# MoE down projection: high and low activation parts side by side for experts with at most 64 tokens, and a branch around the third pass

## The chip, the core and the metric
The kernel runs on one core of one Trainium2 chip. The metric is the time of one execution on the device in microseconds; the time before is 1982.52 us, the median of 3 runs (1981.83 to 1983.2). Engines are named as the profile names them: PE is TensorE's matmul side and PEld its weight loads, DVE is VectorE, ACT is ScalarE, POOL is GpSimd, SP issues the DMAs.

## The reference, cut to what matters
Two layers of a diffusion backbone work on 256 latent tokens (and 256 context tokens) of width 1024. The last step of the second layer is a mixture of experts, on the latent tokens alone. Each token goes to its two best of 8 experts; each expert is a SwiGLU with 3584 hidden units:

```
logits = h @ router_w + router_b
top_v, top_i = lax.top_k(logits, 2)
top_p = softmax(top_v)
combine = sum(one_hot(top_i, 8) * top_p[..., None], -2)
for e in range(8):
    y = y + combine[:, e:e+1] * ((silu(h @ w_gate[e]) * (h @ w_up[e])) @ w_down[e])
```

All of it is float32. The 256 tokens give 512 token-expert pairs. With the inputs of the reference the experts 0 to 7 get 56, 67, 72, 33, 73, 39, 115 and 57 tokens.

## The kernel before
**Splitting.** A float32 product is made of three TensorE passes on operands of type fp32r. Each operand is split into a high part (a copy in fp32r) and a low part (the rest): `split` (lines 135 to 145) does this for weights, with ACT writing `wh` (line 142) and DVE writing `wl` (line 144). `three` (lines 156 to 160) then issues high x high, high x low and low x high into one PSUM tile. The activations are the stationary operand, the weights the moving one (512 columns).

**Buffers.** Weights come in chunks of 1 MB. `rawtile` hands out the raw buffers in a fixed cycle of nine (six `rawx`, two `raw`, one half of `hT`); SP's queue holds the loads in program order, each waiting until its buffer is free. A chunk gives two weight pairs (`wh`, `wl`). Pairs live in seven buffers each of `wh` and `wl`, used in turn (three in `whp` and `wlp`, four in `mowx`).

**The expert loop.** `moe` (line 956) routes: `pc` holds the number of tokens of each expert on every partition, `pos` the place of each token in its expert's list, or -1. `gather_x` (line 1025) builds `Gr`, a 0/1 matrix (token by place) from a comparison of `pos` with a row of places, and brings the tokens of two experts at a time into places 0 to 127 by matmuls with it; `gather_g` turns `Gr` over for the way back (`gt`) and fetches the combination weights (`cw`). A token's row goes to each place whose column of `Gr` holds a 1. `experts` (line 1132) then runs over 8 experts and 7 blocks of 512 hidden units, 56 blocks in all. A block is:

- the up product `pu` (`wblock`: 4 pairs, 24 matmuls), `Silu` of the gate product on ACT (line 1158) and its product with `pu` on DVE (`sg`, line 1159);
- the gate product of the next block (`wblock`, 24 matmuls), in the middle of which (`MID`) `hidden` (line 1079) transposes `sg` by 4 matmuls and splits it into `hx`: high part on ACT (line 1086), low part on DVE (line 1087);
- `down` (line 1090): 4 pairs, each used by 6 matmuls (three passes for each half of the 1024 output columns), into two PSUM tiles `dn` that are kept over the 7 blocks.

After an expert's last block `scatter` (line 1111) evicts `dn` with the weights `cw`, as high and low part `ye` (ACT line 1117, DVE line 1118), and brings it back to token order by 16 matmuls with `gt` (line 1125), which DVE adds into `hT` (line 1128); these are spread over the next block.

An expert with more than 128 tokens would need a second turn: line 1021 loads the largest count into a register of every engine and line 1022 runs the whole loop again inside a conditional if it is over 128. With these inputs it is skipped.

**What sets the order.** The program is written in text order; a planner of the tile framework then orders the instructions of each engine's queue by a timing model of its own, and adds the semaphores. So the queues differ from the text: the transposes of `hidden` may stand earlier than `MID` says, and weight halves of later blocks ahead of an eviction. A conditional is a unit to the planner: nothing from outside is interleaved with what is in it, and the text behind it becomes a new stretch with its own order, on every engine. On the skipping path each engine with work inside waits until its earlier work is counted as finished, and then adds what the skipped work would have counted. Each engine runs its own queue in order, without a common clock.

Of the kernel before, what the change touches and what calls it, by code (L numbers as in the profile page):

```python
# [9 lines left out]
F32 = mybir.dt.float32  # L10
F32R = mybir.dt.float32r
I32 = mybir.dt.int32
AF = mybir.ActivationFunctionType
OP = mybir.AluOpType
# [3 lines left out]
P = 128  # L18
# [3 lines left out]
LAT = 256  # L22
# [3 lines left out]
NE = 8  # L26
FFE = 3584
NB = FFE // 512
CW = 31
EPS = 1e-6  # L30
PADW = 286

C_ID, C_ONE, C_UT, C_IO, C_TJ, C_HALF = 0, 128, 256, 384, 640, 644
CSTW = 648
# [38 lines left out]
class Kernel:  # L73
# [44 lines left out]
    def mm(self):  # L118
        return self.psm.tile([P, 512], F32, name="mm", tag="mm")
# [594 lines left out]
            nc.vector.tensor_tensor(r, od, r, OP.mult)  # L714
            nc.vector.tensor_tensor(yt[1][:, 2 + c, y0:y0 + 256], r[:, 0:256], r[:, 256:512], OP.add)

    MID = 5
    WCYC = 3
    CUTS = ((0, 256), (256, 512))
    ORDER = ("crgp0SBqmt1b23M", "kcrgp0SBqt123")  # L720
# [235 lines left out]
    def moe(self):  # L956
        nc = self.nc
# [4 lines left out]
        W = self.small  # L962
# [19 lines left out]
        ps = self.tp()  # L982
# [4 lines left out]
        pc = self.po()  # L987
# [1 line left out]
        nc.tensor.matmul(pc[:, 0:96], self.ones, selp[:, 1], start=False, stop=True)  # L989
        nc.vector.scalar_tensor_tensor(t1, ps[:, 0:192].rearrange("p (t n) -> p t n", t=2)[:, :, 0:NE], 1.0, sel, OP.add, OP.mult)  # L990
        nc.vector.tensor_scalar(pos, t1, -1.0, None, OP.add)
        self.pos = pos
        utp = self.pool(self.ctx, "utp", 1)
        uth = utp.tile([P, 2, D], F32R, name="uth")
        utl = utp.tile([P, 2, D], F32R, name="utl")
# [29 lines left out]
    def gather_x(self, ep, chunk, first=False):  # L1025
        nc = self.nc
        xh, xl = self.u8((P, KT, 2, P), F32R, "xh"), self.u8((P, KT, 2, P), F32R, "xl")
        Gr = self.mos.tile([P, 2, 256], F32R, name="Gr", bufs=1)
        iota = self.cst[:, C_IO + chunk * P:C_IO + (chunk + 1) * P]
        for i in range(2):  # L1030
            for t in range(2):
                nc.vector.tensor_scalar(Gr[:, t, i * P:(i + 1) * P], iota, self.pos[:, t, ep + i:ep + i + 1], None, OP.is_equal)

        def step(q):
            ps = self.dn() if first and q % 2 else self.tp()
            for r in range(2):
                c = slice(r * 256, r * 256 + 256)
                k = 2 * q + r
                for j, ut in enumerate((self.uth, self.utl)):
                    for t in range(2):  # L1040
                        nc.tensor.matmul(ps[:, c], ut[:, t, k * P:(k + 1) * P], Gr[:, t, :], start=j + t == 0, stop=j + t == 2)
                b = self.mcol(1, 24 + k, 0)
                v = ps[:, c].rearrange("p (i n) -> p i n", i=2)
                nc.scalar.activation(xh[:, k], v, AF.Identity, bias=b)
                nc.vector.scalar_tensor_tensor(xl[:, k], v, b, xh[:, k].bitcast(F32), OP.add, OP.subtract)

        steps = [lambda q=q: step(q) for q in range(4)]
        return [(xh[:, :, i], xl[:, :, i]) for i in range(2)], Gr, steps
# [27 lines left out]
                    mid()  # L1076
        return ps

    def hidden(self, g):
        nc = self.nc  # L1080
        tp = self.tp()
        for f in range(4):
            nc.tensor.transpose(tp[:, f * P:(f + 1) * P], g[:, f * P:(f + 1) * P], self.ident)
        hx = self.mos.tile([P, 2, 4, P], F32R, name="hx", tag="hx", bufs=1)
        t3 = tp.rearrange("p (f n) -> p f n", f=4)
        nc.scalar.copy(hx[:, 0], t3)  # L1086
        nc.vector.tensor_tensor(hx[:, 1], t3, hx[:, 0].bitcast(F32), OP.subtract)  # L1087
        return hx

    def down(self, e, b, pd, hx):  # L1090
        hh, hl = hx[:, 0], hx[:, 1]
        end = e == NE - 1 and b == NB - 1
        w = []

        def part(j, f, n):
            wh, wl = w[2 * j + f]
            c = slice(n * 512, n * 512 + 512)
            self.three(pd[n], hh[:, 2 * j + f], hl[:, 2 * j + f], wh[:, 0, c], wl[:, 0, c],
                       b == 0 and j == 0 and f == 0, b == NB - 1 and j == 1 and f == 1)

        for j in range(2):
            w += self.weights(self.A["w_moed"][e, 2 * b + j], (2, D))
            for f in range(2):
                for n in range(1 if end else 2):
                    part(j, f, n)
        if end:
            for j in range(2):
                for f in range(2):
                    part(j, f, 1)

    def scatter(self, pd, G, last):
        nc = self.nc
# [19 lines left out]
    def experts(self, chunk, first=None):  # L1132
# [22 lines left out]
        for n, (e, b) in enumerate(blocks):  # L1155
            pu = self.wblock(X[e], e, b, 1)
            g = self.sg.tile([P, 512], F32, name="sg")
            nc.scalar.activation(g, pg, AF.Silu)
            nc.vector.tensor_tensor(g, g, pu, OP.mult)
            hx = []  # L1160
            for f in later[0:2]:
                f()
            if e % 2 and b == 1 and e + 1 < NE:
                gather = prep(e + 1)
            if b:
                next(gather, None)
            if n + 1 < len(blocks):
                e1, b1 = blocks[n + 1]
                pg = self.wblock(X[e1], e1, b1, 0, lambda: hx.append(self.hidden(g)))
            else:  # L1170
                hx.append(self.hidden(g))
            for f in later[2:4]:
                f()
            later = []
            if b == 0:
                pd = [self.dn() for _ in range(2)]
            self.down(e, b, pd, hx[0])
            if b == NB - 1:
                later = self.scatter(pd, G[e], e == NE - 1)
        for f in later:  # L1180
# [112 lines left out]
```

## Time and profile before
| | |
|---|---|
| median of 3 runs | 1982.52 us |
| profiled execution: span from first to last instruction | 1977.4 us |
| TensorE busy (share of the span) | 1909.9 us (97%) |
| DVE, ACT busy | 1472.1 us (74%), 1065.3 us (54%) |
| expert loop | from about 957 us to the end |
| down matmuls (`dn<-wh,hx`, `dn<-wl,hx`, `dn<-wh,hx`) | 3 x 448 |

The profiled execution is one of its own, told by its span; what the runs' times hold beside the span is the start and the end of the program. The page gives busy times, the stage tables split them by stretches of time, the timelines list instructions in order of time with their start, duration and line, and what an engine sat idle for stands in brackets with the engine that released it. A matmul's record lasts longer than the distance to the next one, because matmuls are pipelined: distances between starts tell the pace.

### The profile page before, as it was taken

How to read it: one execution, taken by the hardware profiler on the slowest of the kernel's cores; microseconds unless marked ns; L12 is line 12 of the kernel's file. 1: busy time of each engine (PE TensorE's matmuls, PEld its weight loads, DVE VectorE, ACT ScalarE, POOL GpSimd, SP SyncE). 2: the span in 40 equal slices, each digit the busy share in tenths (PEclk: the TensorE clock that was granted, in tenths of full speed). 3: DMA queues.
4: the chain of work that ended last, by engine and by line, in shares of the span. 5: the costliest groups of instructions: out<-in, count | busy, mean ns of one | idle time of the engine just before them, and what ended most of it. 6: DMA issues, size and time to landing. Idle time of an engine off the chain costs nothing.

```text
span 1977.4 us, 24739 instructions
## 1 busy us (share of the span) xinstructions
PE 1909.9 (97%) x9422; PEld 1517.8 (77%) x9422; DVE 1472.1 (74%) x1930; ACT 1065.3 (54%) x1371; POOL 106.6 (5%) x98
## 2 busy tenths in 40 slices
PE   5999999999999999999899999999999999999996
PEld 2886548878878789877788888888878888788785
DVE  4875344785545358756799999889898898988986
ACT  3322334332222234435678777767776777767773
POOL 2100011110110020011000000000000000000000
PEclk9999999999999999999999999999999999999998
DMA  8220355455544213226698999998999999999991
GB/s 313 101 94 25 132 198 217 162 213 192 189 151 156 79 60 133 96 74 250 233 367 324 336 348 346 349 352 328 346 342 364 368 339 341 340 356 368 348 367 52
DMA packets 71806, 481.97 MB, mean 244 GB/s; under 512 B 8320, under 2 KB 12544, under 8 KB 14464
## 3 DMA queue, kind: packets, MB, share of 16 engines
q1 hardware_dynamic: 71680, 480.32, 65.1%
q8 instruction: 76, 1.25, 0.3%
q14 instruction: 50, 0.41, 0.1%
HBM read 479.24 MB, written 1.05 MB: 243 GB/s over the span
## 4 chain that ended last, share of the span: by engine, by line
issue 53%; PE 43%; DVE 2%; POOL 1%; ACT 1%; DMA 0%; POOLq 0%; SPq 0%; DVEq 0%; ACTq 0%
PE mm L159 9%; PE mm L158 9%; PE mm L160 9%; PE dn L158 2%; PE dn L160 2%; PE dn L159 2%; PE po L553 2%; PE dn L540 1%; PE mm L207 1%; PE tp L549 1%; PE dn L685 1%; DVE wl L144 1%; POOL rms L706 1%; PE dn L564 0%; PE tp L372 0%
## 5 line engine op out<-in xcount | busy, mean ns | idle before, releaser
L144 DVE TENSOR_TENSOR wl<-rawx,wh 128x1024 fp32r<-128x1024 f32 x496 | 586.7, 1221 | 87.8 <-ACT wh L142 84.7
L142 ACT CAST wh<-rawx 128x1024 fp32r<-128x1024 f32 x496 | 497.2, 1049 | 182.3 <-PE mm L159 92.6
L159 PE MATMUL mm<-wl,xh 128*128 128x512 f32 x896 | 356.1, 397 | 0.0
L158 PE MATMUL mm<-wh,xh 128*128 128x512 f32 x896 | 354.8, 396 | 0.0
L160 PE MATMUL mm<-wh,xl 128*128 128x512 f32 x896 | 352.3, 393 | 0.0
L142 ACT CAST wh<-raw 128x1024 fp32r<-128x1024 f32 x220 | 224.1, 1050 | 192.8 <-PE mm L159 106.8
L144 DVE TENSOR_TENSOR wl<-raw,wh 128x1024 fp32r<-128x1024 f32 x220 | 263.0, 1224 | 49.7 <-ACT wh L142 47.6
L158 PE MATMUL mm<-uh,wh 128*128 128x512 f32 (+1 forms) x664 | 245.2, 372 | 4.7 <-ACT uh L396 3.6
L159 PE MATMUL mm<-ul,wh 128*128 128x512 f32 (+1 forms) x664 | 244.8, 371 | 1.0 <-POOL ul L397 0.5
L160 PE MATMUL mm<-uh,wl 128*128 128x512 f32 (+1 forms) x664 | 244.3, 370 | 0.0
L159 PEld LDWEIGHTS mm<-wl,xh 128*128 128x128 f32 x896 | 168.6, 188 | 40.3 <-DVE wl L144 3.3
L158 PEld LDWEIGHTS mm<-wh,xh 128*128 128x128 f32 x896 | 168.5, 188 | 36.6
L160 PEld LDWEIGHTS mm<-wh,xl 128*128 128x128 f32 x896 | 168.6, 188 | 36.3
L159 PE MATMUL dn<-wl,hx 128*128 128x512 f32 x448 | 177.4, 396 | 2.2 <-DVE wl L144 2.2
L160 PE MATMUL dn<-wh,hx 128*128 128x512 f32 x448 | 172.7, 393 | 0.3 <-DVE hx L1087 0.3
L158 PE MATMUL dn<-wh,hx 128*128 128x512 f32 x448 | 160.0, 396 | 0.7 <-ACT hx L1086 0.7
L158 PEld LDWEIGHTS mm<-uh,wh 128*128 128x128 f32 x664 | 126.0, 191 | 33.4 <-ACT uh L396 5.3
L159 PEld LDWEIGHTS mm<-ul,wh 128*128 128x128 f32 x664 | 126.1, 191 | 25.8 <-POOL ul L397 2.1
L160 PEld LDWEIGHTS mm<-uh,wl 128*128 128x128 f32 x664 | 126.1, 191 | 22.0 <-issue 1.1
L159 PEld LDWEIGHTS dn<-wl,hx 128*128 128x128 f32 x448 | 84.3, 188 | 23.5 <-DVE wl L144 4.8
L158 PEld LDWEIGHTS dn<-wh,hx 128*128 128x128 f32 x448 | 84.2, 188 | 22.5 <-ACT hx L1086 4.1
L160 PEld LDWEIGHTS dn<-wh,hx 128*128 128x128 f32 x448 | 83.5, 188 | 19.3 <-DVE hx L1087 1.6
(289 smaller groups left out, 2602.9 us busy)
## 6 DMA issues: line engine op xcount, KB each, us to landing
rawx<-w_moe SPq DMA_DIRECT2D x148, 1024.0 KB, 6.8
rawx<-w_moed SPq DMA_DIRECT2D x72, 1024.0 KB, 6.7
raw<-w_moe SPq DMA_DIRECT2D x54, 1024.0 KB, 6.6
raw<-w_mod SPq DMA_DIRECT2D x29, 1024.0 KB, 4.9
rawx<-w_mod SPq DMA_DIRECT2D x19, 1024.0 KB, 5.5
raw<-w_moed SPq DMA_DIRECT2D x19, 1024.0 KB, 7.1
hT<-w_moed SPq DMA_DIRECT2D x18, 1024.0 KB, 6.8
hT<-w_moe SPq DMA_DIRECT2D x17, 1024.0 KB, 6.7
```

The source lines that it names most:

```text
L142: nc.scalar.copy(h, r)
L144: nc.vector.tensor_tensor(l, r, h.bitcast(F32), OP.subtract)
L158: mm(ps, ah, bh, start=first, stop=False)
L159: mm(ps, ah, bl, start=False, stop=False)
L160: mm(ps, al, bh, start=False, stop=last)
L207: nc.tensor.matmul(ps[32 * j:32 * j + 32, :], self.cT[:, k, :], w[:, j, :], start=start, stop=stop)
L540: nc.tensor.matmul(sc, self.qT[r0:r0 + 64, hp, q0 + qt * P:q0 + (qt + 1) * P], self.kT[r0:r0 + 64, hp, :], start=True, stop=True)
L549: nc.tensor.transpose(tp[:, kt * P:(kt + 1) * P], p[:, kt * P:(kt + 1) * P], self.ident)
L553: nc.tensor.matmul(po[r0:r0 + 64, 0:256], self.vt[:, kt, h * 64:h * 64 + 64], pt[:, kt, :], start=kt == 0, stop=kt == 3)
L685: nc.tensor.matmul(sc[:, t * 256:t * 256 + 256], self.rqk[r, 1, o0 + t * P:o0 + (t + 1) * P], self.rqk[r, 0, o0:o0 + 256], start=True, sto ...
L706: nc.gpsimd.tensor_tensor(m, m, self.half.unsqueeze(2).to_broadcast([P, 4, 2]), OP.pow)
```

## The change
The experts with at most 64 tokens (`few`) get each token twice, at place p and at place p + 64: the second half of `Gr`'s columns compares with `pos2 = pos + 64 * few`. In `hidden`, the upper 64 columns of the high part are then overwritten by t - few * high (`self.few` holds -few): for a small expert that is the low part, for a large one the sum with 0, the exact transposed value in fp32r. One stationary tile so holds high and low parts side by side; two passes (with `wh` and `wl`) give all products, and the scatter adds the two places of a token. The third pass (`rest`) is put behind the first 16 matmuls of a block and inside a conditional on TensorE alone, on the expert's count, which is loaded into a register once per expert. In the second turn (chunk 1) the third pass is always done. The special order of the very last block is dropped, and `MID` goes from 5 to 4.

```diff
-    MID = 5
+    MID = 4
...
-        self.pos = pos
+        few, pos2 = W("few", (NE,)), W("pos2")
+        nc.vector.tensor_scalar(few, pc[:, 0:NE], HALF + 0.5, None, OP.is_lt)
+        for t in range(2):
+            nc.vector.scalar_tensor_tensor(pos2[:, t], few, float(HALF), pos[:, t], OP.mult, OP.add)
+        self.pos = (pos, pos2)
+        self.few = W("nfew", (NE,))
+        nc.gpsimd.tensor_scalar(self.few, few, -1.0, None, OP.mult)
+        self.cnt8 = W("cnt8", (NE,), I32)
+        nc.vector.tensor_copy(self.cnt8, pc[:, 0:NE])
+        self.many = {}
...
-                nc.vector.tensor_scalar(Gr[:, t, i * P:(i + 1) * P], iota, self.pos[:, t, ep + i:ep + i + 1], None, OP.is_equal)
+                for h in range(2):
+                    c = slice(h * HALF, h * HALF + HALF)
+                    ps = self.pos[h if chunk == 0 else 0]
+                    nc.vector.tensor_scalar(Gr[:, t, i * P:(i + 1) * P][:, c], iota[:, c], ps[:, t, ep + i:ep + i + 1], None, OP.is_equal)
...
         nc.scalar.copy(hx[:, 0], t3)
+        if chunk == 0:
+            b = hx[:, 0, :, HALF:]
+            nc.vector.scalar_tensor_tensor(b, b.bitcast(F32), self.few[:, e:e + 1], t3[:, :, HALF:], OP.mult, OP.add)
         nc.vector.tensor_tensor(hx[:, 1], t3, hx[:, 0].bitcast(F32), OP.subtract)
...
-    def down(self, e, b, pd, hx):
+    def down(self, e, b, pd, hx, chunk):
...
             for f in range(2):
-                for n in range(1 if end else 2):
-                    part(j, f, n)
-        if end:
-            for j in range(2):
-                for f in range(2):
-                    part(j, f, 1)
+                wh, wl = w[2 * j + f]
+                for n in range(2):
+                    c = slice(n * 512, n * 512 + 512)
+                    k = 2 * j + f
+                    mm(pd[n], hh[:, k], wh[:, 0, c], start=b == 0 and k == 0, stop=False)
+                    mm(pd[n], hh[:, k], wl[:, 0, c], start=False, stop=b == NB - 1 and k == 3)
+
+        def rest():
+            for n in range(2):
+                for k in range(4):
+                    mm(pd[n], hl[:, k], w[k][0][:, 0, n * 512:n * 512 + 512], start=False, stop=True, skip_group_check=True)
+
+        if chunk:
+            rest()
+        else:
+            with self.tc.If(self.many[e] > HALF):
+                rest()
...
             if b == 0:
                 pd = [self.dn() for _ in range(2)]
+                if chunk == 0:
+                    self.many[e] = nc.tensor.value_load(self.cnt8[0:1, e:e + 1], min_val=0, max_val=LAT)
```

## Rows read from the trace of the kernel before

**Rows 1.** The page: busy us, share of the span and instructions of each engine.
```profile
PE 1909.9 (97%) x9422; PEld 1517.8 (77%) x9422; DVE 1472.1 (74%) x1930; ACT 1065.3 (54%) x1371; POOL 106.6 (5%) x98
```
**Rows 2.** The stage table, 800 us of the expert loop: busy us (instructions), PE clock, DMA share, GB/s.
```profile
1100.00:1900.00 800.00, 797.42 (x3622) 647.46 (x3621) 709.76 (x721) 584.63 (x664) 0.00 (x0) 1.00 0.93 349
```
**Rows 3.** Timeline of PE, one block: start us, us, engine, line, operation, count.
```profile
1306.06 0.40 PE L160 MATMUL mm<-wh,xl 128*128 128x512 f32 x1
...
1309.51 0.39 PE L160 MATMUL mm<-wh,xl 128*128 128x512 f32 x1
1309.74 0.64 PE L158 MATMUL dn<-wh,hx 128*128 128x512 f32 x2
...
1315.33 0.39 PE L158 MATMUL mm<-wh,xh 128*128 128x512 f32 x1
```
**Rows 4.** Timeline of DVE, the same block: idle us before it and its releaser in brackets.
```profile
1303.84 0.69 DVE L1159 TENSOR_TENSOR sg<-sg,mm 128x512 f32<-128x512 f32 x1 [1.49 <-PE mm L160]
1304.45 1.22 DVE L144 TENSOR_TENSOR wl<-rawx,wh 128x1024 fp32r<-128x1024 f32 x1
1305.58 2.35 DVE L144 TENSOR_TENSOR wl<-raw,wh 128x1024 fp32r<-128x1024 f32 x2
1307.85 0.68 DVE L1087 TENSOR_TENSOR hx<-tp,hx 128x512 fp32r<-128x512 f32 x1
1308.45 2.35 DVE L144 TENSOR_TENSOR wl<-raw,wh 128x1024 fp32r<-128x1024 f32 x2
1311.51 4.63 DVE L144 TENSOR_TENSOR wl<-rawx,wh 128x1024 fp32r<-128x1024 f32 x4 [0.70 <-ACT wh L142]
...
1321.03 0.69 DVE L1159 TENSOR_TENSOR sg<-sg,mm 128x512 f32<-128x512 f32 x1 [1.48 <-PE mm L160]
```
**Rows 5.** Groups by line, 1100 to 1900: busy us, mean ns, idle before and releaser.
```profile
L159 PE MATMUL dn<-wl,hx 128*128 128x512 f32 x356 | 141.3, 397 | 2.2 <-DVE wl L144 2.2
L1158 ACT ACTIVATE sg<-mm 128x512 f32<-128x512 f32 x44 | 26.3, 597 | 50.2 <-PE mm L160 50.2
```
**Rows 6.** Line 1022, the existing conditional: queue, operation, ns min/median/max, start.
```profile
L1022 PEldq COMPARE_BRANCH  x1: 3722/3722/3722, 1959.8 to 1959.8; - x1
...
L1022 DVEq COMPARE_BRANCH  x1: 72/72/72, 1960.8 to 1960.8; - x1
L1022 PEldq EVENT_SEMAPHORE  x1: 51/51/51, 1963.6 to 1963.6; - x1
```
**Rows 7.** Line 1021, the register load ahead of it, TensorE's queue.
```profile
L1021 PEldq TENSOR_LOAD <-cnti x1: 490/490/490, 1959.2 to 1959.2; - x1
```
**Rows 8.** Timeline of all engines, last block: TensorE stops for DVE and starts again.
```profile
1951.84 0.68 DVE L1087 TENSOR_TENSOR hx<-tp,hx 128x512 fp32r<-128x512 f32 x1
...
1952.58 0.50 PE L160 MATMUL dn<-wh,hx 128*128 128x512 f32 x1 [0.34 <-DVE hx L1087]
...
1952.91 0.39 PE L158 MATMUL dn<-wh,hx 128*128 128x512 f32 x1
```
**Rows 9.** Timeline of DVE, the change from expert 1 to expert 2.
```profile
1212.12 1.40 DVE L1118 SCALAR_TENSOR_TENSOR ye<-dn,cw,ye 128x512 fp32r<-128x512 f32 x2
...
1217.44 0.87 DVE L1128 SCALAR_TENSOR_TENSOR hT<-tp,mod,hT 128x256 f32<-128x256 f32 x2
```
**Rows 10.** Timeline of PE, scatter matmuls of the last expert.
```profile
1957.31 0.63 PE L1125 MATMUL tp<-gt,ye 128*128 128x256 f32 x4
```
**Rows 11.** Waits of SP's queue, 980 to 1950: us in total, times, longest.
```profile
SPq L132 <- DVE wl L144: 816.1, 314, 7.7
```
**Rows 12.** The page: DMA issues, KB each, median us from issue to landing.
```profile
rawx<-w_moe SPq DMA_DIRECT2D x148, 1024.0 KB, 6.8
```
**Rows 13.** Timeline of DVE, the end of the routing.
```profile
950.45 0.17 DVE L991 TENSOR_SCALAR pos<-t 128x16 f32<-128x16 f32 x1
```
**Rows 14.** Timeline of ACT, the change from expert 1 to expert 2.
```profile
1209.89 1.05 ACT L142 CAST wh<-rawx 128x1024 fp32r<-128x1024 f32 x1 [0.33 <-PE dn L160]
1210.85 1.26 ACT L1117 ACTIVATE ye<-dn,cw 128x512 fp32r<-128x512 f32 x2
```

More of the change, by code (lines that the diff above doesn't have):

```diff
@@ L31 @@
 PADW = 286
+HALF = 64
 C_ID, C_ONE, C_UT, C_IO, C_TJ, C_HALF = 0, 128, 256, 384, 640, 644
@@ L1077, in wblock, with hidden @@
         return ps
-    def hidden(self, g):
+    def hidden(self, g, e, chunk):
         nc = self.nc
@@ L1086, in hidden @@
         nc.scalar.copy(hx[:, 0], t3)
+        if chunk == 0:
+            b = hx[:, 0, :, HALF:]
+            nc.vector.scalar_tensor_tensor(b, b.bitcast(F32), self.few[:, e:e + 1], t3[:, :, HALF:], OP.mult, OP.add)
         nc.vector.tensor_tensor(hx[:, 1], t3, hx[:, 0].bitcast(F32), OP.subtract)
         return hx
-    def down(self, e, b, pd, hx):
+    def down(self, e, b, pd, hx, chunk):
+        mm = self.nc.tensor.matmul
         hh, hl = hx[:, 0], hx[:, 1]
-        end = e == NE - 1 and b == NB - 1
         w = []
[L1095 to L1099, printed above, removed]
         for j in range(2):
@@ L1168, in experts @@
                 e1, b1 = blocks[n + 1]
-                pg = self.wblock(X[e1], e1, b1, 0, lambda: hx.append(self.hidden(g)))
+                pg = self.wblock(X[e1], e1, b1, 0, lambda: hx.append(self.hidden(g, e, chunk)))
             else:
-                hx.append(self.hidden(g))
+                hx.append(self.hidden(g, e, chunk))
             for f in later[2:4]:
@@ L1176, in experts @@
                 pd = [self.dn() for _ in range(2)]
-            self.down(e, b, pd, hx[0])
+                if chunk == 0:
+                    self.many[e] = nc.tensor.value_load(self.cnt8[0:1, e:e + 1], min_val=0, max_val=LAT)
+            self.down(e, b, pd, hx[0], chunk)
             if b == NB - 1:
```

## Prediction, written before the result was known
> **What bounds the kernel now.** I read the page's busy times first, then the stage table, then one block of the expert loop on each engine, then the waits. TensorE is busy for 97% of the span [rows 1]. In the expert loop it is busy for 797.4 of 800 us at a granted clock of 1.00 (the 2.4 GHz level), VectorE (DVE) for 709.8, ScalarE (ACT) for 584.6, and the DMA engines for a share of 0.93 at 349 GB/s [rows 2]. So TensorE bounds this stage, but DVE has only 11% to give.
>
> One block (one expert, 512 of its hidden units) runs from one `sg` product to the next, 1303.84 to 1321.03: 17.19 us [rows 4]. TensorE never stops in it: gate and up matmuls start 0.230 us apart (15 starts from 1306.06 to 1309.51), down matmuls 0.233 us apart (24 from 1309.74 to 1315.33) [rows 3]. DVE follows: the low half of a weight pair takes 1.22 us, the next starts 1.135 us later; `sg` takes 0.61 us to the next start, the low half of `hx` 0.60. That makes 12 x 1.135 + 0.61 + 0.60 = 14.8 us of 17.19. The rest is idle at two places: 1.49 us ahead of `sg`, for a TensorE result, and 0.70 us ahead of the third down pair [rows 4]. TensorE waited 2.2 us in all for the down pass's low halves over 800 us [rows 5], so it runs close behind DVE there.
>
> **What the change does here.** The reference's router on its inputs gives the experts 56, 67, 72, 33, 73, 39, 115 and 57 tokens: four (0, 3, 5, 7) have at most 64 ("small"), four don't ("large").
>
> *Removed.* Each small expert drops 8 matmuls in each of 7 blocks: 4 x 7 x 8 = 224, x 0.233 = **-52.2 us**.
>
> *The branch.* The trace has one conditional. Its compare-and-branch takes 72 ns on DVE and 3722 ns on TensorE, where it jumps over a whole second expert loop; an event of 51 ns follows [rows 6]. The new jump passes 8 matmuls. On the skipping side the semaphore count of the skipped work has to be made up, which can only be done when the sixteenth matmul has ended, so the pipeline empties. A matmul lasts 0.39 us against a start every 0.23 (+0.16); after a wait TensorE starts 0.06 us behind its releaser (`hx` at 1951.84 + 0.68 = 1952.52, start 1952.58) and the second matmul comes 0.33 instead of 0.23 us later (+0.10) [rows 8]; the event adds 0.05 [rows 6], a short jump as much. Together 0.42; I take 0.45 x 28 = **+12.6 us**. Bounds: 0.1 (the emptying alone) and 3.7 us (each jump like the long one), 3 to 104 us. I stay near the low end because the target lies a few instructions ahead. The Trainium skill (Advanced Engine Details and Errata, Control Flow Timing) gives about 108 ns for a compare-and-branch and about 51 ns for a jump; with both exposed the term would be 28 x (0.37 + 0.16), an estimate of 14.8 us. The trace agrees only for DVE's short one; its long one is far slower. Large experts take the branch too, but TensorE's sequencer gets there while matmuls are queued: 0, at most 28 x 0.1. The eight register loads (490 ns [rows 7]) hide the same way: 0, at most 3.9.
>
> *DVE's new operation.* 56 times DVE rewrites the upper half of `hx` (128 x 256, from PSUM). The nearest row is line 1128's form, two in 0.87 us [rows 9], so about 0.40 each in a queue; ends 0.2 and 0.6: DVE's block becomes 15.2 us. A small block on TensorE becomes 17.19 - 8 x 0.233 + 0.45 = 15.8. So DVE still fits, with 0.6 us to spare instead of 2.4, and what matters is its queue order.
>
> *The order of the down pass.* Until now each weight pair fed 6 matmuls (1.40 us) in the down pass; in the new first 16, each feeds 4 (0.93 us), faster than DVE's 1.135. In the order of [rows 4], the fourth low half is written 0.61 + 3 x 1.135 + 0.40 + 0.60 + 3 x 1.135 + 1.22 = 9.64 us after `sg` starts. TensorE reaches the down pass 5.90 us after it (1309.74) and wants that half for its fourteenth matmul, at 5.90 + 13 x 0.233 = 8.93: 0.71 us late, in every block, large ones too. If one more pair is queued ahead of `sg`, into the idle 1.49 us, it is 8.50 and nothing waits. Bounds 0 to 0.71, x 56 = 0 to 40 us. The queue will be written anew for a DVE that has more to do, and the idle time of the row is longer than one pair, so I take a value near the low end, 0.20: **+11.2 us**. The high parts of all four pairs are also held until the end of the branch, but of seven buffers three stay free, and DVE's next three pairs last 3.4 us: 0. MID = 4 asks for the transposes 3 matmuls earlier to make room for the rewrite: 0; if they catch `sg` unfinished, at most 0.1 x 56.
>
> *Scatter.* Once per expert DVE has 1.40 + 8 x 0.40 = 4.6 us more [rows 9], TensorE 16 short matmuls (four in 0.63 us [rows 10], about 0.12 apart), 1.9. Of the 2.7 us between, one large block takes up its spare 2.0, a small one its 0.6: 4 x 0.7 + 4 x 2.1 = **+11 us**. Bounds 0 to 22.
>
> *Loads.* A block loads 6.3 MB; 349 GB/s at share 0.93 [rows 2] would be 375 at 1, 16.8 us per block, slower than 15.8. But SP waits 816 us of the loop for DVE to free buffers [rows 11], so loads run ahead by the nine raw buffers less the 6.8 us to land [rows 12], some 15 us. Small experts eat 7 us of it each, large ones give 3 back: 0, at most +5.
>
> *Ends.* Three small DVE operations stand ahead of the first `Gr` (about 0.17 each [rows 13]) and twice as many `Gr`: +1. The last block loses its split by halves but is 1.9 us shorter: -0.5.
>
> Sum: -52.2 + 12.6 + 11.2 + 11 + 0.5 = -16.9. The profiled execution spans 1977.4 us; the median of the runs is 1982.5, so 5.1 lie around the span. 1977.4 - 16.9 + 5.1 = **1965.6 us**.
>
> **Rivals.**
> 1. *The evictions come first* (slower). A conditional cuts every engine's queue in two: nothing from behind it can be queued ahead of it. Now ACT makes the next expert's weight halves before it evicts `dn` (1209.89 before 1210.85 [rows 14]). In the new text the eviction stands right behind the branch and the weights after it. If ACT takes them in that order, it waits for the end of the down pass and then needs 1.26 (two evictions) and 1.05 [rows 14] with 0.60 (`Silu` [rows 5]) between, and DVE 1.22, until the first low half is there: 4.1 us, of which TensorE's scatter fills about 0.7. 7 x 3.4 = 24. With the down pass 0.71 late in each block (40) the sum is -52.2 + 12.6 + 40 + 24 + 0.5 = +25: **2007 us**. It decides once lateness per block exceeds 0.5 us with the evictions in front. For it: the order shown is one a queue without cuts allows. Against: the idle ahead of `sg` leaves room.
> 2. *DVE hides all but the drain* (much faster): -52.2 + 7 + 5 + 0.5 = -40: **1943**. For it: DVE's 0.6 us per block. Against: the in-order waits of [rows 4].
> 3. *A jump costs a fetch.* At 3.7 us each, 104 in place of 12.6: +75, **2057**; at 1.05 us nothing is left of the gain. For it: the long jump [rows 6]. Against: it passed thousands of instructions. The Trainium skill (Runtime: NRT & Kernel Launch, Instruction fetch mechanics) says a taken branch whose target is outside the fetched window stalls for the fetch; by it these jumps would stall only where one crosses the window's end.
> 4. *No change*: lateness adds to 35 to 43 us: **1978.5 to 1986.5**. That the branch doesn't skip at all (counts read wrong) belongs near rival 1; hardly likely.
>
> **How the numbers follow.** Forecast (1953 to 1978.5) 0.40; rival 2 (under 1953) 0.15; no change 0.10; rival 1 0.29; rival 3 0.06. About 0.2% (4 us) is what a measurement can tell from none. Faster 0.55, same 0.10, slower 0.35. The range must reach into rival 1 on one side and rival 2 on the other: 1943 to 2012; the likeliest case's own range is 1953 to 1978.5.
>
> **What would show it.** 1120 down matmuls instead of 1344. In small experts' blocks, about 15.8 us from `sg` to `sg`, with a gap of about 0.45 us ahead of each next up pass and, in large experts, 17.2 to 17.9. DVE busy for 95% or more of small blocks. Gaps ahead of the down pass's low-half matmuls, released by DVE, tell the order's price; gaps of 3 us after each expert's last down pass, released by ACT or DVE, would be rival 1; jumps of over 1 us on TensorE's sequencer rival 3. The forecast is wrong if large blocks lengthen by as much as small ones shorten.

## The result and the profile after

The changed kernel takes 2003.95 us (median of 4 runs, 2002.48 to 2006.01) against 1982.86 (4 runs, 1981.83 to 1983.92): a ratio of 1.0115, interval 1.0102 to 1.0127. It was forecast to come 17 us faster and came 21 slower. That is close to the price of rival 1 (2007), but by luck: of rival 1's two parts, lateness came, and more of it than rival 1 had counted, and the 24 us for evictions did not. The sign that the prediction gave for being wrong came as well: the large experts lengthened by more than the small ones shortened. The profiled execution spans 2003.3 us, 25.9 more than before.

The page's busy times, then the sum of a stage table over the 800 us of [rows 2] (its means are of eight windows of 100 us), both of the changed kernel:

```profile
PE 1909.9 (95%) x9198; PEld 1465.3 (73%) x9198; DVE 1493.4 (75%) x2006; ACT 1056.3 (53%) x1371; POOL 107.0 (5%) x99
```
```profile
sum 800.00, PE 779.07 PEld 591.00 DVE 704.61 ACT 560.59 POOL 0.00; mean PE 97.38 PEld 73.87 DVE 88.08 ACT 70.07 POOL 0.00
```

There are 224 matmuls fewer than in [rows 1], as counted. But TensorE's busy time by the records is the same 1909.9 us, though its work is 224 x 0.233 = 52 us less. So some 52 us of short stalls count as busy, because a record (0.39 us) outlasts the usual distance between two starts (0.23), and the longer span is idle time on top. In the stage TensorE now shows 20.9 us of idle time where it had 2.6 [rows 2].

One plain block of a large expert (no gather, no scatter), `sg` to `sg`, first DVE and ACT, then TensorE's down pass; brackets give the idle us before a row and its releaser:

```profile
1277.20 0.69 DVE L1179 TENSOR_TENSOR sg<-sg,mm 128x512 f32<-128x512 f32 x1 [2.61 <-PE mm L161]
1277.81 3.49 DVE L145 TENSOR_TENSOR wl<-rawx,wh 128x1024 fp32r<-128x1024 f32 x3
1281.21 0.47 DVE L1102 SCALAR_TENSOR_TENSOR hx<-hx,nfew,tp 128x256 fp32r<-128x256 f32 x1
1281.72 0.69 DVE L1103 TENSOR_TENSOR hx<-tp,hx 128x512 fp32r<-128x512 f32 x1
1282.33 2.35 DVE L145 TENSOR_TENSOR wl<-rawx,wh 128x1024 fp32r<-128x1024 f32 x2
1284.91 2.36 DVE L145 TENSOR_TENSOR wl<-rawx,wh 128x1024 fp32r<-128x1024 f32 x2 [0.24 <-ACT wh L143]
...
1295.58 0.69 DVE L1179 TENSOR_TENSOR sg<-sg,mm 128x512 f32<-128x512 f32 x1 [2.39 <-PE mm L161]
```
```profile
1283.35 0.60 ACT L1178 ACTIVATE sg<-mm 128x512 f32<-128x512 f32 x1 [1.59 <-PE mm L161]
1283.84 2.00 ACT L143 CAST wh<-rawx 128x1024 fp32r<-128x1024 f32 x2
```
```profile
1283.15 0.63 PE L1117 MATMUL dn<-wh,hx 128*128 128x512 f32 x2
1283.61 0.72 PE L1118 MATMUL dn<-wl,hx 128*128 128x512 f32 x2
...
1285.29 0.63 PE L1117 MATMUL dn<-wh,hx 128*128 128x512 f32 x2
1286.20 0.72 PE L1118 MATMUL dn<-wl,hx 128*128 128x512 f32 x2 [0.28 <-DVE wl L145]
1286.76 0.62 PE L1117 MATMUL dn<-wh,hx 128*128 128x512 f32 x2
1287.33 0.74 PE L1118 MATMUL dn<-wl,hx 128*128 128x512 f32 x2
1287.90 2.03 PE L1123 MATMUL dn<-wh,hx 128*128 128x512 f32 x8
1289.77 0.39 PE L159 MATMUL mm<-wh,xh 128*128 128x512 f32 x1
```

DVE's queue has the order of [rows 4] with the rewrite (L1102) put in. The fourth low half is ready at 1284.91 + 2.36 = 1287.27, 10.07 us after `sg`; TensorE starts the pair that needs it at 1287.33. The first 16 matmuls take 4.75 us (1283.15 to 1287.90) in place of 16 x 0.233 = 3.73, so 1.02 more, and the 8 of the third pass follow behind, 1.87. The block lasts 18.38 us against 17.19 [rows 4]. Of the difference of 1.19 us the 16 matmuls hold 1.02; the rest lies in the 48 matmuls of the gate and up products, which take 11.31 us here and 11.13 in the block of [rows 4]. No run tells why. DVE then stands idle for 2.39 us ahead of the next `sg`: a loop of two engines in which each waits for the other in turn.

The weight-load side of TensorE tells it best (waits from 980 to 1960: us, times, longest):

```profile
PEld dn L1118 <- DVE wl L145: 67.3, 146, 1.5
```

The matmul rows of the same line show 15.6 us and 40 waits. In the block above the loads of all four low-half groups waited, 0.26 to 0.71 us each, but only the third group shows idle time in the matmul rows. The others show as starts 0.33 us apart instead of 0.23 (a row of two that lasts 0.72, less 0.39).

Where the 25.9 us lie, from the starts of `sg` in both traces (us from the first `sg` of an expert to that of the next; S has at most 64 tokens, L more):

| | before | after | difference | forecast |
|---|---|---|---|---|
| up to the first `sg` | 970.1 | 974.5 | +4.4 | +1 |
| e0 S | 119.5 | 111.7 | -7.8 | |
| e3, e5 S, with the gather of the next pair | 257.2 | 255.3 | -1.9 | |
| e7 S, 6 blocks | 105.4 | 103.8 | -1.7 | S in all: -25.6 |
| e1, e2, e4, e6 L | 496.7 | 530.1 | +33.3 | L in all: +8.4 |
| behind the last `sg` | 28.4 | 27.9 | -0.5 | -0.5 |

So the forecast missed by 24.9 us in the large experts, by 14.2 in the small ones and by 3.4 at the start.

### The profile page after: what moved, and what is told of

Same layout as the page of the kernel before. It is cut to its first block, busy times and chain, and to the rows that moved or that the text cites. A ratio compares the mean times of both kernels' runs of the same rounds, so it can differ in the third digit from the quotient of the medians.

```text
span 2003.3 us, 24496 instructions
## 1 busy us (share of the span) xinstructions
PE 1909.9 (95%) x9198; PEld 1465.3 (73%) x9198; DVE 1493.4 (75%) x2006; ACT 1056.3 (53%) x1371; POOL 107.0 (5%) x99
## 4 chain that ended last, share of the span: by engine, by line
issue 54%; PE 42%; DVE 2%; POOL 1%; ACT 1%; DMA 0%; POOLq 0%; SPq 0%; DVEq 0%; ACTq 0%
PE mm L160 9%; PE mm L161 9%; PE mm L159 9%; PE dn L159 2%; PE dn L161 2%; PE dn L160 2%; PE po L554 2%; PE dn L541 1%; PE mm L208 1%; PE tp L550 1%; PE dn L686 1%; DVE wl L145 1%; POOL rms L707 1%; PE dn L565 0%; PE tp L704 0%
## 5 line engine op out<-in xcount | busy, mean ns | idle before, releaser
L143 ACT CAST wh<-rawx 128x1024 fp32r<-128x1024 f32 x496 | 490.0, 1048 | 159.8 <-PE mm L160 92.7
L160 PE MATMUL mm<-wl,xh 128*128 128x512 f32 x896 | 360.5, 402 | 4.1 <-DVE wl L145 2.7
L1118 PE MATMUL dn<-wl,hx 128*128 128x512 f32 x448 | 163.2, 429 | 16.4 <-DVE wl L145 15.9
L1117 PE MATMUL dn<-wh,hx 128*128 128x512 f32 x448 | 148.7, 397 | 2.1 <-DVE hx L1102 2.0
L1118 PEld LDWEIGHTS dn<-wl,hx 128*128 128x128 f32 x448 | 71.3, 188 | 74.5 <-DVE wl L145 69.0
L1099 ACT CAST hx<-tp 128x512 fp32r<-128x512 f32 x56 | 32.9, 588 | 130.3 <-PE tp L1096 129.7
L1117 PEld LDWEIGHTS dn<-wh,hx 128*128 128x128 f32 x448 | 83.2, 188 | 23.7 <-ACT wh L143 2.8
L1179 DVE TENSOR_TENSOR sg<-sg,mm 128x512 f32<-128x512 f32 x56 | 38.4, 686 | 72.3 <-PE mm L161 72.2
```

The costliest lines, as they stand in the source:

```text
L143: nc.scalar.copy(h, r)
L160: mm(ps, ah, bl, start=False, stop=False)
L1117: mm(pd[n], hh[:, k], wh[:, 0, c], start=b == 0 and k == 0, stop=False)
L1118: mm(pd[n], hh[:, k], wl[:, 0, c], start=False, stop=b == NB - 1 and k == 3)
```

## The experiments

The theory after the result, here theory 1: the two-pass order asks for a weight pair every 0.93 us, DVE's queue delivers the fourth low half too late, in every block. Rivals: the conditional costs the time (by its drain, its jump or its cut of the queues), or the rewrite added on DVE does. All times are medians; ratios are to the kernel before, run on the same chip. Blocks are plain ones: of expert 6 (L) and expert 7 (S).

| kernel | us | ratio, interval | L block | S block |
|---|---|---|---|---|
| before | 1982.9 | | 17.2 | 17.2 |
| after | 2003.95 | 1.0115 (1.0102 to 1.0127) | 18.4 | 16.9 |
| order_only | 2007.6 | 1.0126 (1.0107 to 1.0145) | 18.2 | 18.2 |
| rewrite_only | 1998.4 | 1.0081 (1.0064 to 1.0097) | 17.4 | 17.4 |
| static_skip | 1989.2 | 1.0037 (1.0025 to 1.0050) | 18.35 | 16.9 |
| if_else | 1995.7 | 1.0071 (1.0052 to 1.0090) | 18.2 | 17.2 |
| early_pair | 1997.5 | 1.0084 (1.0068 to 1.0101) | 18.25 | 16.8 |
| early_order | 2005.1 | 1.0124 (1.0107 to 1.0141) | 18.1 | 18.1 |
| early_rewrite | 1985.4 | 1.0023 (1.0014 to 1.0033) | 17.2 | 17.2 |
| early_if_else | 1972.5 | 0.9958 (0.9944 to 0.9972) | 17.35 | 16.8 |
| late_silu | 1994.3 | 1.0061 (1.0044 to 1.0078) | 18.0 | 16.6 |
| both_pair | 1991.1 | 1.0050 (1.0033 to 1.0066) | 17.15 | 16.4 |
| both_order | 1965.7 | 0.9916 (0.9899 to 0.9933) | 17.0 | 17.0 |
| both_if_else | 1994.5 | 1.0061 (1.0045 to 1.0078) | 17.2 | 16.4 |
| act_pair | 1962.7 | 0.9899 (0.9882 to 0.9916) | 17.2 | 15.8 |
| act_if_else | 1969.4 | 0.9939 (0.9921 to 0.9958) | 17.2 | 15.8 |
| act_static | 1951.9 | 0.9850 (0.9834 to 0.9867) | 17.2 | 15.8 |
| act_before | 1965.1 | 0.9914 (0.9898 to 0.9931) | 17.0 | 17.0 |

### One part at a time

**order_only**: the kernel before, with the changed `down` and an unconditional third pass.
```
-            with self.tc.If(self.many[e] > HALF):
-                rest()
+        rest()
```


> The kernel before with one edit: in each down pass the 16 matmuls of the first two passes come first and the 8 of the third pass behind them, always. No conditional, no places doubled, no rewrite on DVE; all three passes are computed. Theory 1 (the order of the down pass: the first 16 matmuls take a weight pair every 0.93 us, DVE makes one every 1.135 us, so the fourth low half is late in every block): some 0.3 to 0.8 us per block, since DVE's chain is without the rewrite's 0.51 us; 2000 to 2025 us. Rival A (the conditional and what it cuts cost the time): no change, 1979 to 1987. Rival B (the rewrite added on DVE costs it): no change, 1979 to 1987.

2007.6 us: plain blocks lengthen by 1.0 to 1.1 us (0.3 to 0.8 were expected) without a conditional and without the rewrite, with DVE's queue in the order of [rows 4]. This is nearly the whole loss of a large block (18.2 against 18.4 in the changed kernel).

**rewrite_only**: the kernel before, with the rewrite in `hidden` and a factor of 0.
```
+        nc.gpsimd.memset(self.few, 0.0)
...
         nc.scalar.copy(hx[:, 0], t3)
+        b = hx[:, 0, :, 64:]
+        nc.vector.scalar_tensor_tensor(b, b.bitcast(F32), self.few[:, e:e + 1], t3[:, :, 64:], OP.mult, OP.add)
```


> The kernel before with one edit: DVE's rewrite of the upper 64 columns of the high part in every block, with a factor of 0, so that the values stay what they were; the three passes keep their old order, no conditional. Theory 1: the fourth low half comes 0.5 us later but is wanted only by the 20th of 24 matmuls, so TensorE hardly waits: 1981 to 1991 us. Rival A (conditional): 1979 to 1987. Rival B (the rewrite makes DVE late in every block): 0.4 us or more per block, 2003 to 2015.

1998.4 us, a miss on theory 1's side: 7 us above its range. The rewrite moves the *first* low half of the down pass back by 0.5 us as well, and that one had no slack: in a plain block the down pass starts at 1792.92, the half is ready at 1793.34 and its load starts at 1793.39.

```profile
1793.39 0.19 PEld L159 LDWEIGHTS dn<-wl,hx 128*128 128x128 f32 x1 [0.28 <-DVE wl L144]
```

That is 0.26 us per block, the size of the loss (56 x 0.26 = 14.6 of 16.8). The chain was at its limit at both ends, and the prices of the two parts don't add up.

**static_skip**: the changed kernel, with the skip fixed when the program is written.
```
-            with self.tc.If(self.many[e] > HALF):
+        if chunk or e not in (0, 3, 5, 7):
                 rest()
```


> The changed kernel without its conditional: the third pass is left out of experts 0, 3, 5 and 7 when the program is written (with these inputs the same work), always done in the others. Theory 1: the lateness of the down pass stays (about 1.0 us in each large block), what goes is the drain of some 0.42 us in 28 small blocks, if DVE's order lets TensorE use it: 1985 to 2003 us. Rival A (the conditional costs the time, by cutting the queues or by the jump): 1940 to 1965. Rival B (rewrite): 1990 to 2003.

1989.2 us. The plain blocks of experts 6 and 7 stay at 18.35 and 16.9: in expert 7 neither jump nor drain (the wait until the pipeline is empty) costs anything, because the block waits for DVE anyway. In expert 0, where DVE's queue was ahead, the drain does cost. In its first four blocks in the changed kernel the up or gate product starts 0.55 and then 0.31 us behind, in place of 0.23 each, and nothing is made up later; static_skip has no such gap there. The changed kernel, expert 0:

```profile
998.91 0.39 PE L1118 MATMUL dn<-wl,hx 128*128 128x512 f32 x1
999.46 0.47 PE L159 MATMUL mm<-wh,xh 128*128 128x512 f32 x1
999.76 0.39 PE L160 MATMUL mm<-wl,xh 128*128 128x512 f32 x1
```

The 15 us between this and the changed kernel lie in expert 0 (4.1), in expert 1 (3.4) and in the other large experts (2.0 to 2.5 each). These lose 1.0 us in the last block (19.96 us against 18.95), at the change of experts, and 1.0 us in the second block (18.27 against 17.26), which no run explains.

**if_else**: the old order of 24 matmuls in the conditional, two passes in its `Else`.
```
+            with self.tc.If(self.many[e] > HALF) as cmp:
+                passes(True)
+            with cmp.Else():
+                passes(False)
```


> The changed kernel with both orders inside the conditional on TensorE: where the count is over 64 the 24 matmuls in the old order (six to a weight pair), otherwise the 16 of the two passes. Rewrite, doubled places and conditional stay. Theory 1: large blocks go back from 18.35 to 17.2 to 17.5 us, small ones stay at 16 to 17: 1968 to 1980 us. Rival A (conditional): no better than the changed kernel, 1998 to 2012. Rival B (the rewrite): the same, 1998 to 2012.

1995.7 us, a miss. The planner placed the transposes of `hidden` later, 2.8 us behind `sg` instead of 1.4, and DVE stood still for them (DVE, a large block, `sg` at 1784.48):

```profile
1785.08 2.35 DVE L145 TENSOR_TENSOR wl<-rawx,wh 128x1024 fp32r<-128x1024 f32 x2
1789.02 0.48 DVE L1102 SCALAR_TENSOR_TENSOR hx<-hx,nfew,tp 128x256 fp32r<-128x256 f32 x1 [1.58 <-ACT hx L1099]
```

So this kernel does not show what the order of the matmuls is worth; a new order in the text moved the queues with it.

### One more pair ahead of `sg`

The edit, the same in four kernels: the first gate chunk of the next block is split ahead of the `sg` product, and the transposes go to MID = 2. Two low halves, not three, are left between `sg` and `hx`.
```
+            w0 = None
+            if n + 1 < len(blocks):
+                w0 = self.weights(self.A["w_moe"][blocks[n + 1][0], blocks[n + 1][1], 0, 0], (4, 512))
             nc.scalar.activation(g, pg, AF.Silu)
```
**early_pair**: on the changed kernel. **early_order**: on order_only. **early_rewrite**: on rewrite_only. **early_if_else**: on if_else.

> The changed kernel with one edit of order: the first chunk of the next block's gate weights is split ahead of the sg product, so that DVE's queue has two low halves, not three, between sg and its part of hx, and the transposes go with it (MID 2). The work is the same. Theory 1 (DVE's chain from sg to the fourth low half of the down pass is the limit in every block): that low half comes about 8.6 us after sg, ahead of TensorE's 8.9; plain large blocks fall from 18.35 to 17.2 to 17.5, plain small ones from 16.95 to 15.7 to 16.1; 1945 to 1970 us. Rival A (the conditional, by its cut or its drain): 1995 to 2010. Rival B (the amount of DVE's work, not its place): 1995 to 2006.

> The kernel before with the two passes first and the third behind them, always, as in order_only (2007.6 us), and the same edit of order as early_pair (first gate chunk ahead of sg, MID 2). Theory 1: the lateness goes, 1978 to 1990 us. If the order of the matmuls costs something of its own on TensorE: about 2005.

> The kernel before with DVE's rewrite, as in rewrite_only (1998.4 us), and the same edit of order as early_pair. Theory 1: the 0.26 us that TensorE waits in each block for the first low half of the down pass goes: 1978 to 1988 us. If the rewrite costs by its time on DVE or by contention: about 1998.

> The kernel if_else (1995.7 us: old order of the 24 matmuls for large experts, two passes for small, both inside the conditional) with the same edit of order as early_pair; the transposes no longer stand 13 matmuls behind sg. Theory 1: plain large blocks 17.2 to 17.5, plain small ones 15.7 to 16.1; 1945 to 1970 us. Rival A (the conditional): 1985 to 2000.

early_rewrite came in at 1985.4 us with blocks of 17.2: there DVE's chain was the cause. But early_pair (1997.5) and early_order (2005.1) kept blocks of 18.1 to 18.25, far above their ranges: theory 1, DVE's chain alone, falls. The trace of early_pair shows a second chain, on ACT (a large block; `sg` at 1790.27, the down pass from 1796.09):

```profile
1793.27 2.00 ACT L143 CAST wh<-hT 128x1024 fp32r<-128x1024 f32 x2
1796.29 0.60 ACT L1181 ACTIVATE sg<-mm 128x512 f32<-128x512 f32 x1 [1.02 <-PE mm L161]
1796.78 4.83 ACT L143 CAST wh<-rawx 128x1024 fp32r<-128x1024 f32 x5
```
```profile
1797.49 0.64 PE L1118 MATMUL dn<-wl,hx 128*128 128x512 f32 x2
1797.96 0.64 PE L1117 MATMUL dn<-wh,hx 128*128 128x512 f32 x2
1799.13 0.73 PE L1118 MATMUL dn<-wl,hx 128*128 128x512 f32 x2 [0.53 <-DVE wl L145]
```

ACT makes two high halves of the down weights, then stands idle 1.02 us for `Silu`, which waits for the end of the gate product, and only then makes the third. The first two pairs run at full pace; the third low half cannot be ready before the gate product's end plus 0.5 (`Silu`), 1.0 (high half) and 1.2 (low half). The old order wants it for its 15th matmul, 14 x 0.233 = 3.3 us into the down pass, the new one for its 11th, 10 x 0.233 = 2.3 us.

early_if_else (1972.5), whose large blocks keep the old order, gains at once: 17.35 us. It still ends 2.5 us above its range, for its small blocks stay at 16.8 instead of 15.7 to 16.1.

### `Silu` behind the fourth high half as well

Theory 2: two chains of nearly one length, DVE's from `sg` and ACT's through `Silu`, set the end of the 16 matmuls; only taking away both helps. `Silu` gets a bias of zero that depends on the fourth high half:
```
+            if j == 1:
+                self.zb = self.sm.tile([P, 1], F32, name="zb", tag="zb", bufs=2)
+                self.nc.gpsimd.tensor_scalar(self.zb, w[3][0][:, 0, 0:1].bitcast(F32), 0.0, None, OP.mult)
...
-            nc.scalar.activation(g, pg, AF.Silu)
+            nc.scalar.activation(g, pg, AF.Silu, bias=self.zb)
```
**late_silu**: this alone, on the changed kernel. **both_pair**, **both_order**, **both_if_else**: on early_pair, early_order and early_if_else.

> The changed kernel; Silu gets a bias of zero that POOL writes after the fourth high half of the block's down weights is made, so ACT's queue has all four high halves ahead of Silu, not two. Theory 2 (two chains of nearly the same length set the end of the first 16 matmuls: DVE's from sg, and on ACT the Silu that waits for the gate product ahead of the third high half): with ACT's chain gone DVE's is left, some 9.8 us in place of 10.06; plain large and small blocks fall by 0.1 to 0.4 us only: 1990 to 2001 us. Theory 1 as it stood (DVE's chain alone): the same or no change. If ACT's Silu alone is the limit: blocks of 17.3 and 15.9, 1950 to 1970.

> The changed kernel with both edits of order: the first gate chunk ahead of sg (as in early_pair, 1997.5 us) and Silu behind the fourth high half (as in late_silu). Theory 2: both chains are shorter than what TensorE asks for: plain large blocks 17.2 to 17.5, plain small ones 15.7 to 16.1; 1945 to 1970 us. If the conditional costs the time, or DVE's amount of work: 1990 to 2000.

> The kernel before with the two passes first and the third behind them, always (order_only 2007.6, with the first gate chunk ahead of sg 2005.1 us), and now both edits of order. Theory 2: lateness gone, plain blocks 17.2 to 17.4; 1977 to 1990 us. If the order of the matmuls has a price of its own on TensorE: 2000 to 2007.

> early_if_else (1972.5 us) with Silu behind the fourth high half as well. Theory 2: what is left is in small blocks (16.83 us in plain ones), where the two passes ask for pairs faster than they come behind Silu: they fall to 15.7 to 16.1, large ones by 0.1; 1942 to 1960 us. Otherwise: 1968 to 1976.

late_silu: 1994.3, blocks 0.3 to 0.4 us shorter, as theory 2 had it. both_order: 1965.7, far below its range; the new order of the matmuls by itself costs TensorE nothing (act_before below, with the old order and the same two edits, takes 1965.1). both_pair has the large blocks that theory 2 gave (17.15), but at 1991.1 missed its time, and so did both_if_else (1994.5): the first block of an expert took up to 24.8 us in the one and 27.7 in the other. What starts it is the experiment's own helper on POOL (both_pair, expert 2):

```profile
1218.08 4.76 POOL L1114 TENSOR_SCALAR zb<-wh 128x1 f32<-128x1 f32 x1 [18.07 <-ACT wh L143]
```
```profile
1218.14 4.62 DVE L145 TENSOR_TENSOR wl<-rawx,wh 128x1024 fp32r<-128x1024 f32 x4
```
```profile
1222.87 0.69 ACT L1186 ACTIVATE sg<-mm,zb 128x512 f32<-128x512 f32 x1 [4.94 <-POOL zb L1114]
```

A second thing follows in the same block. TensorE stands idle for 2.79 us, and its granted clock, 1.00 until then, is 0.50 (the 1.2 GHz level) from 1223.69 to 1230.52. The eight matmuls of the third pass, 2.03 us elsewhere, take 3.31. The two rows of PE, then a window of 24 us with its mean PE clock, 0.86, behind the engines:

```profile
1224.54 0.79 PE L159 MATMUL mm<-wh,xh 128*128 128x512 f32 x1 [2.79 <-ACT wh L143]
1227.69 3.31 PE L1126 MATMUL dn<-wh,hx 128*128 128x512 f32 x8
```
```profile
1212.00:1236.00 24.00, 20.18 (x80) 15.60 (x79) 17.76 (x22) 12.77 (x14) 4.76 (x1) 0.86 0.77 277
```

So part of the loss at these changes of expert is the clock's. The expert loops of the kernel before and of the changed kernel hold no such stretch.

**The helper on ACT itself**: one column in 0.20 us, in place of POOL.
```
-                self.nc.gpsimd.tensor_scalar(self.zb, w[3][0][:, 0, 0:1].bitcast(F32), 0.0, None, OP.mult)
+                self.nc.scalar.mul(self.zb, w[3][0][:, 0, 0:1].bitcast(F32), 0.0)
```
**act_pair**: on both_pair. **act_if_else**: on both_if_else. **act_static**: act_if_else with the conditional replaced by `passes(chunk or e not in (0, 3, 5, 7))`. **act_before**: both edits of order on the kernel before, and nothing of the change.

> both_pair (1991.1 us), with the zero that holds Silu back written by ACT itself behind the fourth high half, not by POOL, whose write of one column took 0.21 to 4.76 us. Theory 2: the first blocks of experts fall from 20.6 to 24.8 us to about 19.3, plain small blocks from 16.45 to 15.8 to 16.1, plain large ones stay at 17.2: 1952 to 1972 us. If the boundaries cost by the conditional's cut of the queues: 1980 to 1991.

> both_if_else (1994.5 us) with the zero written by ACT. Theory 2: 1943 to 1962 us, plain blocks 17.2 (large) and 15.8 to 16.1 (small). If the two orders inside the conditional cost by themselves: 1972 or more.

> act_if_else without its conditional: which experts take two passes (0, 3, 5 and 7) is written into the program, the same work with these inputs. What it is below act_if_else is the conditional's whole price once nothing covers it. Working of the prediction (0.45 us for each of 28 jumps that skip): 10 to 14 us below, plain small blocks 15.4 to 15.6. If the drain stays hidden even now: within 4 us of it.

> The kernel before with both edits of order alone (first gate chunk ahead of sg, Silu behind the fourth high half by ACT's zero); 24 matmuls in the old order, three passes, no conditional. If TensorE was at its floor before (the reading of the trace of before): 1977 to 1985 us. By both_order (1965.7 us, with plain blocks of 16.98 us): 1960 to 1970.

act_pair: 1962.7, and the blocks that the prediction had worked out for a queue without lateness, 17.2 and 15.8. The down pass of a large block runs at full pace, 16 matmuls in 1773.71 - 1769.99 = 3.72 us:

```profile
1769.99 0.63 PE L1120 MATMUL dn<-wh,hx 128*128 128x512 f32 x2
...
1773.26 0.62 PE L1121 MATMUL dn<-wl,hx 128*128 128x512 f32 x2
1773.71 2.03 PE L1126 MATMUL dn<-wh,hx 128*128 128x512 f32 x8
```

A small block of act_pair with the conditional, and one of act_static without, at the step from the down pass to the next up pass:

```profile
1893.70 0.62 PE L1121 MATMUL dn<-wl,hx 128*128 128x512 f32 x2
1894.47 0.47 PE L159 MATMUL mm<-wh,xh 128*128 128x512 f32 x1
1894.78 0.47 PE L160 MATMUL mm<-wl,xh 128*128 128x512 f32 x1
1895.09 0.39 PE L161 MATMUL mm<-wh,xl 128*128 128x512 f32 x1
```
```profile
1882.66 0.63 PE L1122 MATMUL dn<-wl,hx 128*128 128x512 f32 x2
1883.13 0.39 PE L159 MATMUL mm<-wh,xh 128*128 128x512 f32 x1
1883.71 0.51 PE L160 MATMUL mm<-wl,xh 128*128 128x512 f32 x1 [0.19 <-DVE wl L145]
1884.06 0.40 PE L161 MATMUL mm<-wh,xl 128*128 128x512 f32 x1
```

With the skip, the next matmul starts 0.54 us after the one before (1893.93, the second of its row) and the one after it 0.31 later, in place of 0.23 each: a drain of 0.39 us, as in expert 0 above. The third comes 0.31 later as well, so 0.47 us are lost in all. Without the skip TensorE runs on and meets DVE's next low half too early: starts 0.58 and 0.35 us apart lose the same 0.47 us one matmul later. Both blocks last 15.77 us. A window of just that block of act_static (busy us and instructions by engine, PE clock, DMA share, GB/s) shows who sets it:

```profile
1873.60:1889.37 15.77, 15.58 (x69) 12.29 (x68) 15.51 (x16) 12.86 (x15) 0.00 (x0) 1.00 1.01 416
```

DVE is busy for 15.51 of 15.77 us.

act_if_else came in at 1969.4, above its range of 1943 to 1962, though its plain blocks are the 17.2 and 15.8 that were expected. Its trace has four stretches of 3.41 us in the expert loop with a granted clock of 0.50, each where TensorE had just stood idle for 1.97 to 2.31 us at the change of an expert or in expert 1. One of them (columns as above, PE clock behind the engines):

```profile
1224.82:1228.23 3.41, 3.41 (x10) 2.63 (x9) 3.41 (x4) 1.11 (x2) 0.00 (x0) 0.50 0.80 267
```

Its four runs lie 7 us apart, the slower the lower their mean granted clock (1965.6 us at 0.988, 1972.6 at 0.983).

act_static came 17.5 us below act_if_else, more than the 10 to 14 expected, though the plain blocks are alike. Of the 14.2 us between the two profiled executions 11.0 lie in the first three experts, the rest mostly at the start and in expert 7. Up to some 6 us of it are the clock's, by an estimate: in 3.41 us at 0.50, with starts 0.43 us apart, there is room for 7 matmuls fewer than at 0.23, 1.6 us each time. So the 17.5 us are not the price of the jumps alone. act_pair, which has the conditional around the third pass only, lies 10.8 us above act_static.

act_before is the control that the others need: 1965.1 us, not the 1977 to 1985 of a TensorE at its floor. The two edits of order take 17.8 us off the kernel before: plain blocks fall from 17.2 to 17.0, the first block of experts 3 to 7 from 19.5 to 18.4, and the first `sg` comes 3.1 us earlier. So TensorE, which by its records never stopped in a plain block [rows 3], was not at its floor. With the edits on both sides, the change is worth 1962.7 - 1965.1 = -2.4 us (1962.0 to 1963.2 against 1964.9 to 1966.4, both on one chip). act_static, which knows the small experts beforehand and has no conditional, lies 13.3 us below act_before. So most of what the change could give seems to go to the conditional and what hangs on it; act_static also keeps the old order in the large experts, whose plain blocks take the same 17.2 us in both.

## Why the prediction was wrong, step by step

- **Removed matmuls**: 224, right. Their 52.2 us never came back whole, since small blocks turned from TensorE to DVE.
- **The branch**: the drain is 0.39 us, forecast 0.45. As a term of the sum, 28 times on the path, it was wrong: in expert 7 nothing of it is on the path, as static_skip and act_static show, and in the first four blocks of expert 0 all of it is. The conditional's whole price, some 15 us in the changed kernel (2003.95 - 1989.2), comes near the forecast 12.6 by luck, for more than half of it lies in large experts, where 0 was forecast. Rival 3 is out: the row below (form, ns min/median/max) holds the compare that skips, 202 to 343 ns in each of 28 small blocks, and two compares in each of 28 large ones, 65 to 71 and 169 to 292 ns; all lie beside queued matmuls.

```profile
L1128 PEldq COMPARE_BRANCH  x84: 65/169/343, 979.2 to 1979.9; - x84
```
  The Trainium skill (Advanced Engine Details and Errata, Control Flow Timing) states about 108 ns for it; the one that skips takes about twice that here.
- **The order of the down pass**: the step that failed. The text took 0.20 us of a bound of 0.71, because the idle time ahead of `sg` was longer than one pair and the queue would be written anew. It was not: DVE's queue kept the order of [rows 4], and the idle time stayed where it was, as waiting for TensorE. Plain large blocks show 1.15 to 1.2 us, above the bound. The fourth low half is ready 10.07 us after `sg`, not 9.64: 0.24 us of waiting for ACT and 0.11 more for the rewrite had been left out, and 0.08 because a low half behind a wait doesn't overlap the one before it. It is wanted for the fifteenth matmul (two with `wh`, then two with `wl`), not the fourteenth, which gives 0.23 back: 0.71 + 0.43 - 0.23 = 0.91, and with the slower second start behind a wait (0.10) the 1.02 us of the 16 matmuls. The row that showed the second chain stood in [rows 4]: 0.70 us idle ahead of the third pair, released by ACT. The prediction named it idle time and left it out of its 9.64 us; it was `Silu`, waiting for the gate product ahead of the third high half (ACT, the block of [rows 4]):

```profile
1306.37 2.00 ACT L142 CAST wh<-raw 128x1024 fp32r<-128x1024 f32 x2
1309.94 0.60 ACT L1158 ACTIVATE sg<-mm 128x512 f32<-128x512 f32 x1 [1.58 <-PE mm L160]
1310.44 3.88 ACT L142 CAST wh<-rawx 128x1024 fp32r<-128x1024 f32 x4
```
  Removing both chains takes 2003.95 - 1962.7 = 41 us off the changed kernel, of which 17.8 would come to the kernel before as well.
- **DVE's new operation**: 0.51 us to the next start, forecast 0.40. "DVE still fits" was true of its sum, not of its place: rewrite_only lost 16.8 us.
- **Small blocks**: forecast 15.8, seen 16.9 in the changed kernel and 15.77 in act_pair. What the sum missed altogether is the gather. Experts 3 and 5 are small, but their blocks also bring in the tokens of the next pair, and there the change gives 2 us per expert even with both edits (125.3 against 127.4 in act_before) where 10 had been counted. In expert 3 of act_pair DVE is busy for 117.6 of 125 us and waits for ACT in between: 3.4 us for high halves of weights, some 2.5 for ACT's part of the gather. That these two engines bound those blocks is read from this trace and was not tried by a run.
- **Scatter and rival 1**: the scatter's own +11 us are not to be seen: the first block of a large expert stands 2.0 us above a plain one (20.38 against 18.37) and that of expert 7 2.2, where both stood 2.3 above before (19.5 against 17.2). The changes of expert cost about 1.0 us more with a conditional than without (19.96 against 18.95). One weight pair still stands ahead of the evictions and TensorE has matmuls to do: rival 1's stall of 3.4 us is not there. Its other half, lateness in every block, is what came.
- **Loads**: right in that no wait for a load bounds a plain block. The 375 GB/s that the text worked out for a full share were too low: DMA reached 416 GB/s in the window above.
- **Start**: +4.4 us instead of +1. Its parts were not told apart, so the cause is open; in act_pair, with the same operations, it is gone (969.0).

## What to carry to other kernels

A change that makes the bounding engine eat its operands faster must be weighed against when the *last* operand of the group is ready, along every queue that makes it, not against the sum of the other engines' work: an engine with 11% idle time was late in every block. Read the weight-load waits and the brackets of idle time on the helpers as possible chains, not as slack; and before crediting an edit, give the old kernel the same change of order, for here that alone was worth more than the change. A conditional has to be charged for the order of the queues around it, not only for its jumps. Of the versions tried that hold for any counts of tokens, act_pair is the fastest (1962.7 us).

## What the runs showed of the hardware that was not expected

- A POOL operation on one column took 0.21 to 0.23 us in 15 blocks of both_pair and 0.76 or 0.77 in 29, although DVE was at work beside it in all of them. The 29 ended about 0.06 us behind the subtraction that ran when they began, with the next one already started. Six took 4.74 to 4.76 us. Each of these began just as DVE went over from the scatter's additions to a run of four subtractions, and ended only behind the whole run (above: at 1222.84, DVE's run at 1222.76). The Trainium skill (SBUF — State Buffer, SBUF: two separate sides) states an exclusive lock between the two, held for a whole instruction and taken by whichever starts first. The 29 fit it, ending with one subtraction; in the six POOL's wait went over four of DVE's instructions, though its recorded start is the earlier one. Why it got no turn between them is open.
- TensorE's granted clock can fall in the middle of the expert loop. In both_pair and act_if_else it went from 1.00 to 0.50 four times each, for 3.41 or 6.83 us, each time during a wait of TensorE of 1.97 to 2.79 us or within 1.0 us behind it. Not every such wait brought a fall: both_pair waited 2.79 us six times. In the expert loop of the changed kernel, where no wait is longer than 1.02 us, the clock stayed at 1.00.
- Of the planner rather than the chip: the same source text in a new order moved queues that it did not name. In if_else the transposes moved back by 1.4 us and cost DVE 1.58 us per large block.
